# Sliding-window attention in a two-layer trunk: the emptying of its PSUM banks moved ahead in the instruction order

## The chip, the cores and the metric

The kernel runs on one core of a Trainium2 chip. The metric is the device time of one execution in microseconds (us). One core has a matrix engine (TensorE, PE in the profile; its weight loads are PEld), a vector engine (VectorE, DVE), an activation engine (ScalarE, ACT), GpSimd (POOL) and SyncE (SP). TensorE writes its results into PSUM banks, and ScalarE or VectorE copies them out to the on-chip memory SBUF; here such a copy is called an eviction.

## The reference

Input and output are 512 tokens of 1024 features in float32. Each of two layers computes:

```python
h = rmsnorm(x, norm_mix)
z = h @ w_in       # q, k, v of attention; q, k, v, o and gates of the mLSTM; gates A and B
# branch A: 8 query heads over 2 key/value heads of 64, RMS-norm and partial rotary on q and k
scores = einsum('bnqhgd,bnkhd->bnhgqk', qb, kb) * hd**-0.5   # blocks of 128 queries, own and previous block
scores = where(kpos >= 0 & kpos <= qpos & qpos - kpos < 128, scores, -inf)
m = maximum(max(scores), sink);  p = exp(scores - m)
probs = p / (sum(p) + exp(sink - m))
att = einsum('bnhgqk,bnkhd->bnqhgd', probs, vb)
# branch B: hm = chunkwise mLSTM with output gate
mixed = sigmoid(g_a) * (att @ w_att_branch) + sigmoid(g_m) * (hm @ w_m_branch)
x = x + mixed @ w_out
u = relu(rmsnorm(x, norm_ffn) @ w_ff1);  x = x + (u * u) @ w_ff2
```

## The kernel before

Each layer is built by `mixer` (everything up to `mixed @ w_out`) and `mlp`. Float32 products are made of split parts: a matrix is split into a rounded high part and the rest (`h`, `lo`; `wh`, `wl` for weights), and `mm3` issues three products, high by high, high by rest, rest by high. A weight chunk is loaded, and then split by ScalarE (L166) and VectorE (L167). The projections work on 512-column products (`mm` tiles) that collect in five PSUM banks, got from `bank()`.

Attention does not have a stage of its own. It runs as side steps between the projections' products, in 4 blocks of 128 queries by 2 key/value groups, written (b, kv) below. Each side step has a place on a list (`side`), counted in steps of products. Its PSUM space is a second pool of three banks, got from `aux()`, through which all of these pass in turn:

- `q_tr(b)`, `k_tr(b)`: transposes of the queries and keys of a block; evictions with the gains at L585/L586 (queries) and L563 to L566 (keys).
- `att_scores(b, kv, hp)`: scores of two of the group's four heads against the previous and own block; ScalarE copies the previous block's half (L604; for block 0 a fill, L602), VectorE copies the own half under the causal mask (L605, a predicated copy).
- `att_softmax(b, kv)`: works on SBUF only; maximum (L612, VectorE), four exponentials (L618, ScalarE), the sink's exponential (L620), sum and reciprocal (L621, L622), normalising multiplication over 128x512 (L623, VectorE).
- `att_probs(b, kv)`: four transposes (L52) of the normalised weights into one bank, which `split` empties into a high part (L176, ScalarE) and the rest (L177, VectorE). GpSimd masks copies of both for the previous block.
- `att_out(b, kv)`: two or four products with the values into one bank; ScalarE copies the lower half (L649), VectorE adds the head pairs with two additions (L653), and the result is split again (L656, L657).

All matrix products carry line L47 (`pe.matmul`), all transposes L52. The order of the instructions on each engine is fixed when the program is built: a scheduler goes through what is ready and takes it by priority, which normally follows the order of the code. Code under `tc.high_priority()` is put ahead of all else that is ready; `tc.high_priority(n)` raises it by n places. Before the change the raised work includes the weight loads and the weight splits (`lead[0] = 64` within attention). On the chip each engine then runs its own list from first to last, and waits where something isn't there yet.

Of the kernel before, what the change touches and what calls it, by code (L numbers as in the profile page):

```python
# [9 lines left out]
F32R = mybir.dt.float32r  # L10
BF16 = mybir.dt.bfloat16
I32 = mybir.dt.int32
AF = mybir.ActivationFunctionType
ALU = mybir.AluOpType
AX = mybir.AxisListType

P = 128
# [11 lines left out]
NEG = -1.0e30  # L29
# [4 lines left out]
def hybrid_kernel(ctx, tc, x, norm_mix, w_in, att_q_norm, att_k_norm, att_sinks, m_gate_bias,  # L34
# [3 lines left out]
    ve, sc, gp = nc.vector, nc.scalar, nc.gpsimd  # L38
# [23 lines left out]
    def nm(s):  # L62
        uid[0] += 1
        return f"{s}_{uid[0]}"
# [8 lines left out]
    def slot(dt=F32, shape=(P, T)):  # L73
        return now["act"].tile(list(shape), dt, tag="a", name=nm("a"))

    def temp(dt=F32):
        return now["tmp"].tile([P, T], dt, tag="t", name=nm("t"))
# [14 lines left out]
    def aux(shape=(P, T)):  # L92
        return now["paux"].tile(list(shape), F32, tag="aux", name=nm("aux"))
# [4 lines left out]
    def f32(ap):  # L98
        return ap.bitcast(F32)
# [72 lines left out]
    def split(src, scale=None, get=lambda: slot(F32R)):  # L172

        h, lo = get(), get()
        if scale is None:
            last_split[0] = sc.activation(h, src, AF.Copy)  # L176
            last_split[1] = ve.tensor_tensor(lo, src, f32(h), op=ALU.subtract)  # L177
        else:
            last_split[0] = sc.activation(h, src, AF.Copy, scale=scale)  # L179
            last_split[1] = ve.scalar_tensor_tensor(lo, src, scale, f32(h), op0=ALU.mult, op1=ALU.subtract)  # L180
        return h, lo
# [207 lines left out]
    def mixer(l, norm, late, order, phase):  # L389
# [116 lines left out]
        for b in range(NB):  # L506
# [5 lines left out]
                         op=ALU.mult)  # L512
# [15 lines left out]
        for i, v_ in enumerate((v4[:, :NB - 1], dv4)):  # L528
            sc.activation(v2[:, i, :, :, 0, :], v_, AF.Copy, scale=0.5)
            ve.scalar_tensor_tensor(v2[:, i, :, :, 1, :], v_, 0.5, f32(v2[:, i, :, :, 0, :]), op0=ALU.mult,  # L530
                                    op1=ALU.subtract)
# [17 lines left out]
        tri_i = tri_l.bitcast(I32)  # L549
# [21 lines left out]
        def q_tr(b):  # L571


            ps = aux()
            for j in range(4):
                pe.transpose(ps[:, j * P:(j + 1) * P], q_tok[b][:, j * P:(j + 1) * P], ident)
            for j in range(2):
                qT[b, j] = temp(F32R)
                t4 = qT[b, j].rearrange("p (i n t) -> p i n t", n=2, i=2)
                p4 = ps[:, 2 * j * P:2 * (j + 1) * P].rearrange("p (n t) -> p n t", n=2)  # L580
                for i in range(2):
                    r = slice(64 * i, 64 * i + 64)
                    o = slice(64 - 64 * i, 128 - 64 * i)
                    g = gcols[0][r, l:l + 1]
                    sc.activation(t4[r, i], p4[r], AF.Copy, scale=g)  # L585
                    ve.scalar_tensor_tensor(t4[o, i], p4[r], g, f32(t4[r, i]), op0=ALU.mult,  # L586
                                            op1=ALU.subtract)

        def att_scores(b, kv, hp):
            if hp == 0:  # L590
                sps[b, kv] = temp()
            ps = aux()
            for i in range(2):
                c = 2 * i + hp
                lhs = qT[b, kv][:, c * P:(c + 1) * P]
                o = ps[:, i * 2 * P:(i + 1) * 2 * P]
                pe.matmul(o, lhs, kTh[:, kv, b * P:(b + 2) * P], start=True, stop=False)
                pe.matmul(o, lhs, kTl[:, kv, b * P:(b + 2) * P], start=False, stop=True)
            p4 = ps.rearrange("p (h w k) -> p h w k", h=2, w=2)
            dst = sps[b, kv][:, hp * 2 * P:(hp + 1) * 2 * P].rearrange("p (h k) -> p h k", h=2)  # L600
            if b == 0:
                gp.memset(dst, NEG)  # L602
            else:
                sc.activation(dst, p4[:, :, 0, :], AF.Copy)  # L604
            ve.copy_predicated(dst, tri_i.unsqueeze(1).to_broadcast([P, 2, P]), p4[:, :, 1, :])  # L605

        def att_softmax(b, kv):
            sp = sps[b, kv]
# [16 lines left out]
        def att_probs(b, kv):  # L625
            sp = sps[b, kv]
            pt = aux()
            for i in range(4):
                pe.transpose(pt[:, i * P:(i + 1) * P], sp[:, i * P:(i + 1) * P], ident)
            hl = split(pt, get=lambda: temp(F32R))  # L630
            parts[b, kv] = [(hl, v2[:, 0, max(b - 1, 0), kv])]
            if b > 0:


                own = [temp(F32R) for _ in hl]
                for src, dst in zip(hl, own):
                    s3, d3 = (t.rearrange("p (h q) -> p h q", h=4) for t in (src, dst))
                    gp.affine_select(out=d3, in_=s3, compare_op=ALU.is_ge, fill=0.0, base=0,
                                     pattern=[[0, 4], [1, P]], channel_multiplier=-1)
                parts[b, kv].append((own, v2[:, 1, b - 1, kv]))  # L640

        def att_out(b, kv):
            po = aux()
            ls = parts[b, kv]
            for n, (pr, vb) in enumerate(ls):
                for m, p_ in enumerate(pr):
                    pe.matmul(po, vb.rearrange("p i d -> p (i d)"), p_, start=n + m == 0, stop=n == len(ls) - 1 and m == 1)
            low, both = temp(), temp()
            sc.activation(low[0:64, :], po[64:128, :], AF.Copy)  # L649
            p4, l4 = (t[0:64, :].rearrange("p (j i t) -> p j i t", j=2, i=2) for t in (po, low))  # L650
            b3 = both[:, 0:2 * P].rearrange("p (j t) -> p j t", j=2)
            for i in range(2):
                ve.tensor_tensor(b3[64 * i:64 * i + 64], p4[:, :, i, :], l4[:, :, i, :], op=ALU.add)  # L653
            for j in range(2):
                dh, dl = (a[:, b * P:(b + 1) * P] for a in att_acts[2 * kv + j])
                sc.activation(dh, b3[:, j, :], AF.Copy)  # L656
                ve.tensor_tensor(dl, b3[:, j, :], f32(dh), op=ALU.subtract)  # L657
# [182 lines left out]
        for i, (b, kv) in enumerate(units):  # L840
            at = 7 + 1.65 * i
            side += [(at, lambda b=b, kv=kv: att_scores(b, kv, 0)),
                     (at + 1.25, lambda b=b, kv=kv: att_scores(b, kv, 1)),
                     (at + 1.25, lambda b=b, kv=kv: att_softmax(b, kv)),
                     (at + 3.45, lambda b=b, kv=kv: att_probs(b, kv)),
                     (at + 3.45 + 2.2, lambda b=b, kv=kv: att_out(b, kv))]
            if kv == 0 and b + 1 < NB:
                if b + 2 < NB:
                    side += [(at + 1, lambda b=b: k_vec(b + 2)), (at + 1, lambda b=b: q_vec(b + 2))]
                side += [(at + 2 * 1.65 - 1.75, lambda b=b: k_tr(b + 1)), (at + 2 * 1.65 - 2.15, lambda b=b: q_tr(b + 1))]  # L850
# [830 lines left out]
```

## Time and profile before

| | us |
|---|---|
| median of 3 runs | 1278.73 (1278.52 to 1278.82) |
| the profiled execution | 1278.95 |
| its span in the trace | 1277.3 |
| outside the span | 1.65 |
| TensorE busy | 1266.9 (99%) |
| VectorE busy | 1040.4 (81%) |
| ScalarE busy | 793.3 (62%) |
| GpSimd busy | 256.9 (20%) |

The rows are sums over one profiled execution. Engines run side by side, so their times don't add up to the span. Attention of layer 0 lies between about 69 and 133 us of the span, that of layer 1 between about 702 and 766 us. A row of a timeline gives the start, the length, the engine, the line in the kernel, the operation and its tiles with output before input, and in brackets how long the engine had stood idle before it and which work ended that.

### The profile page before, as it was taken

The page shows a single profiled execution, that of the slowest core. Times are in us where ns is not written, and L with a number is a line of the kernel's source. Part 1 is how long each engine was busy: PE and PEld are TensorE (multiplying, and loading weights), DVE is VectorE, ACT ScalarE, POOL GpSimd, SP SyncE. Part 2 cuts the span into 40 slices and gives each one's busy share as a digit, 9 for nine tenths or more (in the row PEclk, how much of TensorE's full clock was granted, in tenths as well). Part 3 has the DMA queues.
Part 4 walks back from the last instruction along what each step waited for, and adds up shares of the span by engine and source line. Part 5 has one row for each costly group of instructions (what it writes and reads, how often), then busy time and mean ns, then how long its engine had stood idle before and what let it go on. Part 6 is the DMA issues. An engine that isn't in the chain of part 4 may idle for free.

```text
span 1277.3 us, 19227 instructions
## 1 busy us (share of the span) xinstructions
PE 1266.9 (99%) x6882; PEld 1088.6 (85%) x6882; DVE 1040.4 (81%) x1654; ACT 793.3 (62%) x1399; POOL 256.9 (20%) x337
## 2 busy tenths in 40 slices
PE   9999999999999999999999999999999999999998
PEld 7877888888889999999888778888888899999987
DVE  4689988688787887969957889876887879879697
ACT  5578579645665666656554885785455656565563
POOL 4513132021003031130114031310300120301210
PEclk9999999999999999999999999999999999999999
DMA  5426372567569898898224254634756697988953
GB/s 157 113 59 158 106 132 75 157 125 156 173 166 208 220 184 213 198 206 214 34 75 117 60 155 108 116 108 139 144 146 185 166 227 187 203 215 191 215 144 99
DMA packets 138927, 193.35 MB, mean 151 GB/s; under 512 B 10568, under 2 KB 79024, under 8 KB 138832
## 3 DMA queue, kind: packets, MB, share of 16 engines
q1 hardware_dynamic: 92992, 129.72, 33.3%
q0 software_dynamic: 45120, 62.00, 30.2%
q8 instruction: 54, 0.88, 0.3%
q10 hardware_dynamic: 720, 0.40, 0.1%
q14 instruction: 41, 0.34, 0.1%
HBM read 188.95 MB, written 2.10 MB: 150 GB/s over the span
## 4 chain that ended last, share of the span: by engine, by line
PE 89%; ACT 5%; DVE 3%; DMA 2%; issue 1%; DVEq 0%; SPq 0%; ACTq 0%
PE mm L47 72%; PE aux L47 14%; PE aux L52 2%; DMA w<-in_w_in_dram 1%; DVE wl L167 1%; ACT t L618 1%; ACT wh L166 1%; ACT t L585 0%; DVE t L653 0%; ACT p L703 0%; DVE t L586 0%; DVE t L177 0%; ACT t L176 0%; DMA x<-in_x_dram 0%; DMA w<-in_w_m_branch_dram 0%
## 5 line engine op out<-in xcount | busy, mean ns | idle before, releaser
L47 PE MATMUL mm<-i,wh 128*128 128x512 f32 (+1 forms) x1280 | 353.6, 363 | 0.0
L1162 ACT ACTIVATE wh<-raw 128x1024 fp32r<-128x1024 f32 x212 | 223.2, 1056 | 178.8 <-PE mm L47 91.8
L1163 DVE TENSOR_TENSOR wl<-raw,wh 128x1024 fp32r<-128x1024 f32 x212 | 255.7, 1221 | 81.0 <-ACT wh L1162 80.8
L47 PEld LDWEIGHTS mm<-i,wh 128*128 128x128 f32 x1280 | 223.2, 189 | 30.4
L47 PE MATMUL mm<-i,wl 128*128 128x512 f32 (+1 forms) x640 | 229.0, 358 | 0.0
L47 PE MATMUL mm<-wh,uh 128*128 128x512 f32 x440 | 171.8, 390 | 0.0
L47 PE MATMUL mm<-wl,uh 128*128 128x512 f32 x440 | 171.7, 390 | 0.0
L47 PE MATMUL mm<-wh,ul 128*128 128x512 f32 x440 | 171.2, 389 | 0.0
L1332 POOL DMA_DIRECT2D raw<-in_w_ff_dram x48 | 62.6, 1311 | 381.2 <-DMA raw<-in_w_ff_dram 246.3
L47 PEld LDWEIGHTS mm<-i,wl 128*128 128x128 f32 x640 | 120.9, 189 | 18.0
L167 DVE TENSOR_TENSOR wl<-w,wh 128x512 fp32r<-128x512 f32 (+1 forms) x144 | 97.3, 678 | 42.9 <-ACT wh L166 42.1
L166 ACT ACTIVATE wh<-w 128x512 fp32r<-128x512 f32 (+1 forms) x144 | 86.4, 604 | 67.4 <-PE mm L47 49.7
L47 PE MATMUL mm<-wh,i 128*128 128x512 f32 (+1 forms) x352 | 101.0, 360 | 1.0 <-ACT wh L166 0.6
L47 PEld LDWEIGHTS mm<-wh,ul 128*128 128x128 f32 x440 | 82.6, 188 | 17.4
L1217 DVE SCALAR_TENSOR_TENSOR x<-mm,ms,x 128x512 f32<-128x512 f32 x126 | 90.6, 745 | 8.1 <-PE mm L47 8.1
L47 PEld LDWEIGHTS mm<-wh,uh 128*128 128x128 f32 x440 | 82.8, 188 | 16.1
L47 PEld LDWEIGHTS mm<-wl,uh 128*128 128x128 f32 x440 | 82.8, 188 | 15.5
L1489 POOL DMA_DIRECT2D raw<-in_w_ff_dram x36 | 43.3, 1204 | 150.6 <-DVE wl L1163 114.9
L47 PEld LDWEIGHTS mm<-wh,i 128*128 128x128 f32 x352 | 62.0, 188 | 11.7 <-ACT i L179 1.1
L47 PE MATMUL aux<-i,wh 128*128 128x256 f32 x384 | 69.5, 283 | 0.0
L47 PE MATMUL aux<-t,wh 128*128 128x256 f32 x384 | 69.5, 283 | 0.0
L47 PE MATMUL mm<-wl,i 128*128 128x512 f32 (+1 forms) x176 | 61.9, 352 | 0.0
(317 smaller groups left out, 2519.4 us busy)
## 6 DMA issues: line engine op xcount, KB each, us to landing
raw<-in_w_ff_dram SPq DMA_DIRECT2D x144, 512.0 KB, 5.0
raw<-in_w_ff_dram POOLq DMA_DIRECT2D x84, 512.0 KB, 8.0
w<-in_w_in_dram SPq DMA_DIRECT2D x112, 256.0 KB, 2.7
a<-in_w_in_dram POOLq DMA_DIRECT2D x32, 256.0 KB, 5.8
qa<-in_w_out_dram POOLq DMA_DIRECT2D x12, 512.0 KB, 5.9
a<-in_w_in_dram SPq DMA_DIRECT2D x16, 256.0 KB, 4.2
w<-in_w_att_branch_dram SPq DMA_DIRECT2D x16, 256.0 KB, 2.8
w<-in_w_m_branch_dram SPq DMA_DIRECT2D x16, 256.0 KB, 2.9
```

Source lines behind the costliest of these rows:

```text
L47: latest[0] = nc.tensor.matmul(*args, **kw)
L52: latest[0] = nc.tensor.transpose(*args)
L166: sc.activation(wh[:, :off], raw[:, :off], AF.Copy)
L167: ve.tensor_tensor(wl[:, :off], raw[:, :off], f32(wh[:, :off]), op=ALU.subtract)
L618: sc.activation(s3[:, i, :], s3[:, i, :], AF.Exp, bias=m[:, i:i + 1], accum_out=den[:, i:i + 1])
L1162: sc.activation(hi, src, AF.Copy)
L1163: ve.tensor_tensor(lo, src, f32(hi), op=ALU.subtract)
L1217: ve.scalar_tensor_tensor(xh[:, cc], ps[i][:, cc], ms[j][:, b:b + 1], xh[:, cc], op0=ALU.mult, op1=ALU.add)
L1332: gp.dma_start(to[h], src(h, i, j), accum_op=ALU.add)
L1489: gp.dma_start(to[h], src(h, i, j), accum_op=ALU.add)
```

## The change

Four groups of evictions of the three auxiliary banks are put under `tc.high_priority()`: those of `q_tr`, of `att_scores`, of `att_probs` and of `att_out`. The evictions of `k_tr`, the softmax and the last split of `att_out` stay as they were.

```diff
@@ q_tr
-                    sc.activation(t4[r, i], p4[r], AF.Copy, scale=g)
-                    ve.scalar_tensor_tensor(t4[o, i], p4[r], g, f32(t4[r, i]), op0=ALU.mult,
-                                            op1=ALU.subtract)
+                    with tc.high_priority():
+                        sc.activation(t4[r, i], p4[r], AF.Copy, scale=g)
+                        ve.scalar_tensor_tensor(t4[o, i], p4[r], g, f32(t4[r, i]), op0=ALU.mult,
+                                                op1=ALU.subtract)
@@ att_scores
-            if b == 0:
-                gp.memset(dst, NEG)
-            else:
-                sc.activation(dst, p4[:, :, 0, :], AF.Copy)
-            ve.copy_predicated(dst, tri_i.unsqueeze(1).to_broadcast([P, 2, P]), p4[:, :, 1, :])
+            with tc.high_priority():
+                if b == 0:
+                    gp.memset(dst, NEG)
+                else:
+                    sc.activation(dst, p4[:, :, 0, :], AF.Copy)
+                ve.copy_predicated(dst, tri_i.unsqueeze(1).to_broadcast([P, 2, P]), p4[:, :, 1, :])
@@ att_probs
-            hl = split(pt, get=lambda: temp(F32R))
+            with tc.high_priority():
+                hl = split(pt, get=lambda: temp(F32R))
@@ att_out
-            sc.activation(low[0:64, :], po[64:128, :], AF.Copy)
             p4, l4 = (t[0:64, :].rearrange("p (j i t) -> p j i t", j=2, i=2) for t in (po, low))
             b3 = both[:, 0:2 * P].rearrange("p (j t) -> p j t", j=2)
-            for i in range(2):
-                ve.tensor_tensor(b3[64 * i:64 * i + 64], p4[:, :, i, :], l4[:, :, i, :], op=ALU.add)
+            with tc.high_priority():
+                sc.activation(low[0:64, :], po[64:128, :], AF.Copy)
+                for i in range(2):
+                    ve.tensor_tensor(b3[64 * i:64 * i + 64], p4[:, :, i, :], l4[:, :, i, :], op=ALU.add)
```

The instructions are the same in number and kind; their places on the engines' lists differ, in attention of both layers and in the same way. The lines of the changed kernel are shifted: L585 is 586, L604/L605 are 606/607, L618 to L623 are 620 to 625, L649 is 655, L653 is 657, L656/L657 are 660/661.

The first place is the softmax of block 1, group 0 in layer 0 (about 88 to 95 us). `t_1013` is its tile of weights with the sums `den_1092`, `aux_1131` the bank of the transposes of the unit before, `aux_1146` that of an `att_out`, `aux_1170` and `aux_1198` banks of scores, `kT_623` the keys, `w_1359` a weight chunk. ScalarE's list before:

```order
L618 ACTIVATE t_1013,den_1092<-t_1013,m_1087 128x128 x4
L620 ACTIVATE es_1090<-es_1090 128x4
L563 ACTIVATE kT_623<-aux_1104,gc_147 64x128
L564 ACTIVATE kT_623<-aux_1104,gc_147 64x128
L176 ACTIVATE t_1136<-aux_1131 128x512
L166 ACTIVATE wh_1361<-w_1359 128x512
L649 ACTIVATE t_1149<-aux_1146 64x512
L604 ACTIVATE t_1114<-aux_1170 128x256
```

And ScalarE's list there now:

```order
L620 ACTIVATE t_1013,den_1092<-t_1013,m_1087 128x128 x2
L176 ACTIVATE t_1136<-aux_1131 128x512
L620 ACTIVATE t_1013,den_1092<-t_1013,m_1087 128x128
L655 ACTIVATE t_1149<-aux_1146 64x512
L620 ACTIVATE t_1013,den_1092<-t_1013,m_1087 128x128
L622 ACTIVATE es_1090<-es_1090 128x4
L563 ACTIVATE kT_623<-aux_1104,gc_147 64x128
L564 ACTIVATE kT_623<-aux_1104,gc_147 64x128
L606 ACTIVATE t_1114<-aux_1170 128x256
L660 ACTIVATE a_632<-t_1150 128x128
L166 ACTIVATE wh_1361<-w_1359 128x512
```

The evictions of `aux_1131` and `aux_1146` now stand between the exponentials of `t_1013`, and the weight split L166 has moved back. VectorE's list at the same place, before:

```order
L621 TENSOR_TENSOR den_1092<-den_1092,es_1090 128x4
L622 RECIPROCAL den_1092<-den_1092 128x4
L623 TENSOR_TENSOR t_1013<-t_1013,den_1092 128x512
L565 SCALAR_TENSOR_TENSOR kT_623<-aux_1104,gc_147,kT_623 64x128
L177 TENSOR_TENSOR t_1137<-aux_1131,t_1136 128x512
L566 CAST kT_623<-kT_623 64x128
L653 TENSOR_TENSOR t_1150<-aux_1146,t_1149 64x256 x2
L605 COPY_PREDICATED t_1114<-tri_l,aux_1170 128x256
```

And VectorE's list there now:

```order
L177 TENSOR_TENSOR t_1137<-aux_1131,t_1136 128x512
L657 TENSOR_TENSOR t_1150<-aux_1146,t_1149 64x256 x2
L623 TENSOR_TENSOR den_1092<-den_1092,es_1090 128x4
L624 RECIPROCAL den_1092<-den_1092 128x4
L565 SCALAR_TENSOR_TENSOR kT_623<-aux_1104,gc_147,kT_623 64x128
L607 COPY_PREDICATED t_1114<-tri_l,aux_1170 128x256
L625 TENSOR_TENSOR t_1013<-t_1013,den_1092 128x512
L566 CAST kT_623<-kT_623 64x128
```

The split of `aux_1131`, the additions on `aux_1146` and the predicated copy on `aux_1170` stood behind the normalising multiplication of `t_1013`; all three stand ahead of it now.

The second place is TensorE's list some ten us later, as the difference of the two lists (minus before, plus now). `mm` tiles are products of the projections, `aux_1307` is a bank for scores of block 1, group 1, and `aux_1317` takes the transposes of that block's group 0, `t_1114`:

```order
 L47 MATMUL mm_936<-i_277,wl_1290 128x512
 L47 MATMUL mm_958<-i_277,wh_1289 128x512
+L47 MATMUL aux_1307<-kT_623,t_1072 128x256 x4
 L47 MATMUL mm_958<-i_278,wh_1289 128x512
 L47 MATMUL mm_958<-i_277,wl_1290 128x512
```

and further on:

```order
 L47 MATMUL mm_1393<-i_115,wh_1361 128x512
 L47 MATMUL mm_1393<-i_114,wl_1362 128x512
-L47 MATMUL aux_1307<-kT_623,t_1072 128x256 x4
 L47 MATMUL mm_1397<-i_114,wh_1361 128x512
 L47 MATMUL mm_1397<-i_115,wh_1361 128x512
 L47 MATMUL mm_1397<-i_114,wl_1362 128x512
 L47 MATMUL mm_1358<-i_114,wh_1411 128x512
+L52 MATMUL aux_1317<-ident,t_1114 128x128 x4
```

The scores `aux_1307` have moved ahead by eleven products, and the transposes `aux_1317` ahead as well.

The third place is VectorE's list around the softmax of block 2, group 1 (`t_1306`, sums `den_1384`); `aux_1437` is the bank of an `att_out`, `aux_1463` and `aux_1491` are banks of scores, `m_1470` takes the maximum of the next unit. Before:

```order
L621 TENSOR_TENSOR den_1384<-den_1384,es_1382 128x4
L622 RECIPROCAL den_1384<-den_1384 128x4
L623 TENSOR_TENSOR t_1306<-t_1306,den_1384 128x512
L653 TENSOR_TENSOR t_1443<-aux_1437,t_1442 64x256 x2
L605 COPY_PREDICATED t_1401<-tri_l,aux_1463 128x256
L605 COPY_PREDICATED t_1490<-tri_l,aux_1491 128x256
```

And now:

```order
L607 COPY_PREDICATED t_1401<-tri_l,aux_1463 128x256
L657 TENSOR_TENSOR t_1443<-aux_1437,t_1442 64x256
L607 COPY_PREDICATED t_1490<-tri_l,aux_1491 128x256
L657 TENSOR_TENSOR t_1443<-aux_1437,t_1442 64x256
L623 TENSOR_TENSOR den_1384<-den_1384,es_1382 128x4
L614 TENSOR_REDUCE m_1470<-t_1401 128x4
L624 RECIPROCAL den_1384<-den_1384 128x4
L661 TENSOR_TENSOR a_637<-t_1443,a_636 128x128
L625 TENSOR_TENSOR t_1306<-t_1306,den_1384 128x512
```

The additions, both predicated copies and the next unit's maximum have gone ahead of the multiplication.

## The prediction

> **What bounds the kernel now.** I read the page's head first, then its busy times and the chain of work that ended last.
>
> ```profile
> span 1277.3 us, 19227 instructions
> PE 1266.9 (99%) x6882; PEld 1088.6 (85%) x6882; DVE 1040.4 (81%) x1654; ACT 793.3 (62%) x1399; POOL 256.9 (20%) x337
> PE 89%; ACT 5%; DVE 3%; DMA 2%; issue 1%; DVEq 0%; SPq 0%; ACTq 0%
> ```
>
> TensorE is busy for 99% of the span, and the chain runs over it for 89%. A reordering that removes no matmul can only win where TensorE stands still: 1277.3 − 1266.9 = 10.4 us in the whole kernel. The next question is how much of this lies where the change moves anything. By the order of instructions, the first row that moves on ScalarE, VectorE or TensorE in layer 0 is one that ran at about 86 us, and the last that matters at about 133; in layer 1 the same rows move between 718 and 765. The table of stretches gives start:end, length, then busy time of PE, PEld, DVE, ACT and POOL, the granted clock, the DMA share and GB/s:
>
> ```profile
> 69.50:85.80 16.30, 15.42 (x85) 12.86 (x84) 13.93 (x35) 11.25 (x35) 0.00 (x0) 1.00 0.22 60
> 85.80:133.00 47.20, 45.79 (x227) 36.08 (x226) 41.16 (x106) 39.87 (x121) 11.92 (x16) 1.00 0.47 124
> 133.00:260.00 127.00, 127.00 (x627) 105.93 (x626) 106.07 (x250) 86.79 (x204) 23.96 (x39) 1.00 0.49 117
> 718.00:765.50 47.50, 46.07 (x229) 36.35 (x228) 41.43 (x107) 40.17 (x121) 12.06 (x16) 1.00 0.49 125
> ```
>
> In the moved stretch PE is idle for 47.20 − 45.79 = 1.41 us of layer 0 and 47.50 − 46.07 = 1.43 of layer 1. Beside it VectorE is busy for 41.16 / 47.20 = 87% and ScalarE for 84%: both are almost full there, so what is put first on them puts something else last. The clock is 1.00, so it decides nothing. From 133 to 260 PE records no idle time at all: a layer that leaves attention late by some tenths stays late, and one that leaves early stays early. What PE waited for, over the whole run (total us, times, longest):
>
> ```profile
> PE aux L52 <- DVE t L653: 1.7, 4, 0.5
> PE aux L47 <- DVE t L605: 1.3, 2, 0.7
> PE aux L47 <- DVE t L653: 0.5, 2, 0.2
> PE aux L52 <- ACT wh L166: 0.3, 2, 0.2
> ```
>
> The 1.7 and 0.5 are waits for an auxiliary bank (three of them) until the head-pair additions of `att_out`, L653, have emptied it. The change aims at these. The 1.3 are waits at the scores for a predicated copy, L605. The prioritised rows include L605, but these two waits (85.24 us in layer 0) lie ahead of the first moved row, in the stretch from 69.50 that loses 16.30 − 15.42 = 0.88 us, so they stay. TensorE's timeline around the waits (start, length, engine, line, operation, tiles; in brackets the wait and who ended it):
>
> ```profile
> 85.24 0.74 PE L47 MATMUL aux<-kT,t 128*128 128x256 f32 x4 [0.67 <-DVE t L605]
> 92.72 0.39 PE L47 MATMUL mm<-i,wh 128*128 128x512 f32 x1
> 93.53 0.63 PE L52 MATMUL aux<-ident,t 128*128 128x128 f32 x4 [0.42 <-DVE t L653]
> 99.11 0.40 PE L47 MATMUL mm<-i,wl 128*128 128x512 f32 x1
> 99.96 0.30 PE L52 MATMUL aux<-ident,kvi 128*128 128x128 f32 x1 [0.45 <-DVE t L653]
> 104.82 0.61 PE L47 MATMUL mm<-i,wh 128*128 128x512 f32 x2
> 105.27 0.39 PE L47 MATMUL mm<-i,wl 128*128 128x512 f32 x1
> 108.22 0.39 PE L47 MATMUL mm<-i,wh 128*128 128x512 f32 x1
> 108.72 0.66 PE L52 MATMUL aux<-ident,t 128*128 128x128 f32 x4
> 113.60 0.40 PE L47 MATMUL mm<-i,wl 128*128 128x512 f32 x1
> 114.23 0.94 PE L47 MATMUL aux<-t,v 128*128 128x512 f32 x3 [0.23 <-DVE t L653]
> 124.78 0.39 PE L47 MATMUL mm<-i,wl 128*128 128x512 f32 x1
> 125.34 0.63 PE L52 MATMUL aux<-ident,t 128*128 128x128 f32 x4 [0.17 <-ACT wh L166]
> ```
>
> Unhindered, a 512-column product starts (105.27 − 104.82) / 2 = 0.225 us after the one before, though each row is 0.39 long. So the true loss at a wait is the distance of two starts less 0.225, and it is larger than the recorded idle: at 93.53 it is 93.53 − 92.72 − 0.225 = 0.58, at 99.96 0.62, at 108.72 0.27, at 114.23 0.40, at 125.34 0.33. Together 2.20 us for layer 0, against 1.41 of recorded idle. That is the most the change can recover per layer.
>
> **The change part by part.** It adds and removes no instruction; work and transfers are the same, and only places in the queues move. On POOL and SyncE two masks and one weight load move past transfers that are needed tens of us later: nothing. Weight splits are moved back behind evictions on ScalarE and VectorE; the split of a weight is needed about 8 us after it (the last one at risk ends at 116.9 and TensorE first reads it at 124.78), so this costs nothing while the delay is under that:
>
> ```profile
> 116.20 0.68 DVE L167 TENSOR_TENSOR wl<-w,wh 128x512 fp32r<-128x512 f32 x1
> ```
>
> What has no such cover is the softmax. Its exponentials (L618), its sum, reciprocal and normalising multiplication (L623) are not raised, and TensorE's next transposes (L52) read what L623 writes. These rows of before show the first place at which the order differs much, ScalarE first, then VectorE; what follows is a replay by hand: the new order, with these durations.
>
> ```profile
> 88.09 0.40 ACT L618 ACTIVATE t<-t,m 128x128 f32<-128x128 f32 x1
> 89.65 0.19 ACT L620 ACTIVATE es<-es 128x4 f32<-128x4 f32 x1
> 90.63 0.60 ACT L176 ACTIVATE t<-aux 128x512 fp32r<-128x512 f32 x1
> 91.25 0.63 ACT L166 ACTIVATE wh<-w 128x512 fp32r<-128x512 f32 x1
> 91.91 0.59 ACT L649 ACTIVATE t<-aux 64x512 f32<-64x512 f32 x1
> 94.20 0.60 ACT L176 ACTIVATE t<-aux 128x512 fp32r<-128x512 f32 x1 [0.47 <-PE aux L52]
> 90.28 0.69 DVE L623 TENSOR_TENSOR t<-t,den 128x512 f32<-128x512 f32 x1
> 91.40 0.69 DVE L177 TENSOR_TENSOR t<-aux,t 128x512 fp32r<-128x512 f32 x1
> 92.54 0.85 DVE L653 TENSOR_TENSOR t<-aux,t 64x256 f32<-64x256 f32 x2 [0.20 <-ACT t L649]
> ```
>
> *Transposes of block 1, group 0 (93.53).* In before the multiplication ended at 90.97, the bank was free at 93.39 when the second addition ended (92.54 + 0.85), and the bank decided. After: two exponentials, L176 (0.60), one exponential, L649 (0.59), the last exponential and the small one. From 88.09 that puts L649 at 90.0 to 90.6 instead of 91.91, and the small exponential's end at 91.1 instead of 89.84. On VectorE the additions end at 91.5, 1.9 us sooner. Sum, reciprocal, one k step and one predicated copy come next, and then the multiplication at 92.6 to 93.3, 2.3 us later than before. TensorE arrives at 93.0, with one more product (0.225) behind it, and starts at about 93.36: it loses 0.37 instead of 0.58. The bank wait has become a data wait. Counting start and product, TensorE is ahead by 0.17 + 0.23 = 0.40.
>
> *The transpose at 99.96.* The bank is that of another `att_out`; its additions move ahead of the multiplication that stood in front of them (98.36, below), and they end about 1.9 us sooner, at 97.9 with TensorE's arrival at 98.9. The wait of 0.62 goes: ahead by 1.02. The rows of this and of the later places:
>
> ```profile
> 98.36 0.69 DVE L623 TENSOR_TENSOR t<-t,den 128x512 f32<-128x512 f32 x1
> 98.97 0.84 DVE L653 TENSOR_TENSOR t<-aux,t 64x256 f32<-64x256 f32 x2
> 117.64 0.69 DVE L623 TENSOR_TENSOR t<-t,den 128x512 f32<-128x512 f32 x1
> 118.25 0.84 DVE L653 TENSOR_TENSOR t<-aux,t 64x256 f32<-64x256 f32 x2
> 119.12 0.78 DVE L605 COPY_PREDICATED t<-tri_l,aux 128x256 f32<-128x256 int32 x2
> 119.24 0.63 PE L52 MATMUL aux<-ident,t 128*128 128x128 f32 x4
> ```
>
> *Scores pulled forward.* The order puts the second scores of block 1, group 1 (aux_1307) some eleven products earlier on TensorE. The bank they take is freed by a predicated copy behind a weight split and the first gate products of VectorE; that copy ends at about 101.0 by the replay, TensorE is there at 100.62 and loses 0.42. The scores of block 2 (aux_1402) come soon after and wait 0.35 for the k part of that block, whose evictions (L563 to L566) aren't raised.
>
> *The later transposes.* At 117.64 the multiplication preceded the additions (118.25) and two predicated copies (119.12); now it follows them and a reduce over a tile of its own size. That is 0.84 + 0.78 + 0.69 = 2.3 us of other work put in front; part of that runs while the exponentials are going on anyway, and in before the multiplication ended 0.9 us ahead of its transposes (at 117.64 + 0.69 = 118.33, against a start at 119.24). I get a loss of 0.52 there. The same working gives 0.58 for block 2, group 0 (108.72 in before), 0.28 for block 3, group 0 (0.33 at 125.34 in before) and 0.25 for its group 1.
>
> *The sum.* Lost per layer in before: 2.20. Lost after: 0.37 + 0.42 + 0.35 + 0.58 + 0.52 + 0.28 + 0.25 = 2.77. That is +0.57. Following TensorE's own position step by step instead, it leaves the last `att_out` of attention 0.40 late, because some of the new losses shorten the next. I take the middle, 0.49, for each of two layers: +1.0 us. The profiled execution took 1278.95, of which 1.65 lie outside the span; with the change 1279.95. The median of the runs is 0.22 under the profiled one, so the forecast is 1279.7. Each of some ten placements of a wait is known to about 0.3 us, independent of the others: about 1 us per layer; as both layers have the same order, the errors add, to 2 us. Its own range is 1277.7 to 1281.3.
>
> A rule that would speak for the change: the Trainium skill, "Perfetto Trace Analysis", section "Optimization Strategy", says that a gap repeating over a stretch of the busiest engine can mean too little PSUM for the next tile. By that rule all bank waits would go and the sum would be rival A's; the trace agrees that L653 ends six of the waits.
>
> **The rivals.** *A, faster: the waits simply go.* The evictions come sooner and the softmax is ready in time all the same. For it: the bank waits at 99.96 and 114.23 had their data long before. Against it: VectorE at 87%, and 2.3 us of delay for L623 at the first transposes alone. It gives 1278.95 − 2 × 2.20 − 0.22 = 1274.3; by recorded idle only, 1278.95 − 1.41 − 1.43 − 0.22 = 1275.9. I take the middle, 1275.1.
>
> *B, slower: the multiplication L623 falls further behind than I worked out.* The mechanism is the queue: an eviction at the head of ScalarE or VectorE whose bank isn't filled yet holds up the exponentials and multiplications behind it. The row at 94.20 shows it in before: L176 stood 0.47 us waiting for TensorE, with a weight split queued after it. With the evictions first, such heads are more frequent, and TensorE's next transposes wait for what is held up, which fills no bank in the meantime. The price is one pass of 0.69 (L623's own size) more at three of the six transposes per layer: 3 × 0.69 × 2 = 4.1 us over the forecast, 1283.8; at all six, 1287.9. It decides from the point where the added losses pass 1.3 us per layer (1278.73 + 2.6 = 1281.3). For it: L623 stands behind L653 in every block of the new order. Against it: the losses I found are each under 0.6. The Trainium skill, "PSUM — Partial Sum Buffer", section "Engine vs sequencer instructions", states that the queues of ScalarE and VectorE are strictly first in, first out; the row at 94.20 agrees.
>
> *C, no effect:* the largest waits (85.24) are ahead of what moves, the rest cancels, 1278.7.
>
> **How the numbers follow.** A measurement of this kernel tells about 0.2%, 2.6 us, from no change: 1276.2 and 1281.3 are the limits. The forecast gets 0.53, A 0.11, B 0.32, C 0.04. B gets more than A because a softmax behind evictions stands in the order itself, while A needs room on an engine that is 87% busy. Faster 0.11 (A), same 0.57 (forecast and C), slower 0.32 (B). The range runs from A's 1275.1, with half of A below it, to 1284.5, just beyond B's price: it leaves out some 0.05 below and 0.13 above.
>
> **What would show it.** Right: the waits of `aux L52` for L653 at 93.53 and 99.96 are gone, and waits of `aux L52` for the multiplication (L625 after the shift of lines) stand in their place, five per layer of 0.2 to 0.6; the waits for the predicated copy at 72 to 86 us are as before; the idle time of 85.8 to 133 is between 1.2 and 2.5 us; the end moves by twice one layer's shift. A would show in that idle time falling under 0.5 us, B in its rising over 2.7 with ScalarE or VectorE standing at evictions. Wrong altogether: a shift that arises outside attention (a late weight, an output transfer), since I put that at nothing.

## The result, and the profile after

The changed kernel takes 1285.46 us (median of 4 runs, 1284.19 to 1285.87), the kernel before 1278.77: ratio 1.0051, 95% interval 1.0039 to 1.0063. It is 6.7 us slower. The forecast was 1279.7, and the range ended at 1284.5.

The profiled execution took 1285.18 us with a span of 1283.5, and TensorE does the same work in it. The stretches of the changed kernel (columns as before):

```profile
PE 1266.8 (99%) x6882; PEld 1087.9 (85%) x6882; DVE 1042.8 (81%) x1654; ACT 792.5 (62%) x1399; POOL 254.1 (20%) x337
69.50:85.80 16.30, 15.31 (x84) 12.64 (x82) 14.09 (x35) 11.13 (x36) 0.00 (x0) 1.00 0.22 63
85.80:133.00 47.20, 43.34 (x215) 33.93 (x216) 40.94 (x104) 38.10 (x117) 10.44 (x15) 1.00 0.46 123
133.00:260.00 127.00, 127.00 (x625) 106.02 (x624) 106.63 (x252) 88.14 (x207) 23.17 (x39) 1.00 0.48 117
```

TensorE's idle time in the stretch of the change has grown from 1.41 to 47.20 − 43.34 = 3.86 us, and it gets through 215 products there instead of 227. VectorE and ScalarE are busy for less time too: no engine has become fuller, all of them wait. Measured from the first scores of a layer (first row `aux<-kT,t`) to the first row `aux<-ones,lf` behind attention, layer 0 takes 78.20 us against 75.51 and layer 1 78.54 against 75.05, so +2.69 and +3.49, where +0.49 was forecast for each. Their sum, 6.18, is all but 0.05 of the difference between the two profiled spans. What TensorE waited for:

```profile
PE aux L52 <- DVE t L625: 6.5, 10, 2.2
PE aux L47 <- DVE t L607: 2.1, 4, 0.8
PE aux L47 <- DVE kT L565: 1.3, 2, 0.6
```

The waits for the additions have gone, and waits for the multiplication (now L625) stand in their place, five per layer, as forecast; but they sum to 6.5 us, and two of them lie far above the 0.2 to 0.6 that was forecast for each. TensorE's timeline shows which of them are large:

```profile
93.92 0.33 PE L52 MATMUL aux<-ident,t 128*128 128x128 f32 x1 [0.18 <-DVE t L625]
101.63 0.39 PE L47 MATMUL aux<-kT,t 128*128 128x256 f32 x1 [0.19 <-DVE t L607]
109.76 0.50 PE L47 MATMUL aux<-kT,t 128*128 128x256 f32 x2 [0.63 <-DVE kT L565]
114.22 0.52 PE L52 MATMUL aux<-ident,t 128*128 128x128 f32 x3 [0.33 <-DVE t L625]
120.75 0.63 PE L52 MATMUL aux<-ident,t 128*128 128x128 f32 x4 [0.36 <-DVE t L625]
127.88 0.63 PE L52 MATMUL aux<-ident,t 128*128 128x128 f32 x4 [1.46 <-DVE t L625]
132.08 0.63 PE L52 MATMUL aux<-ident,t 128*128 128x128 f32 x4 [0.59 <-DVE t L625]
763.64 0.63 PE L52 MATMUL aux<-ident,t 128*128 128x128 f32 x4 [2.19 <-DVE t L625]
```

By the distance of starts the loss is 0.16 to 0.17 more than each bracket. At 127.88, block 3, group 0, it is 1.62 us in layer 0, and 2.35 at the same place in layer 1 (763.64). The chain of waits, followed back from there (start, length, what):

```profile
114.35 0.61 DVE wl L167
114.97 0.02 SPq L155
115.02 6.88 DMA w<-in_w_in_dram
121.98 0.10 ACT wh L166
122.52 0.48 ACT t L620 x2
```

The chain leaves the bank evictions altogether. A weight chunk, issued at 115.02, lands after 6.88 us. ScalarE has its split L166 at the head of its list and waits 2.48 us for it, and the exponentials of block 3 (L620) stand right behind the split. (Of the 2.48 us, 0.71 would be there anyway: in the run below with the transfers out of the way, the same split waits that long for TensorE.)

```profile
121.98 0.63 ACT L166 ACTIVATE wh<-w 128x512 fp32r<-128x512 f32 x1 [2.48 <-DMA w<-in_w_in_dram]
```

The weight itself is needed much later. In the kernel before, the same chunk was issued at 113.39 and landed after 2.6 us, and its split came 5 us after that, without a wait for it:

```profile
DMA to landing us min/median/max: 2.6/2.6/2.6
121.08 0.63 ACT L166 ACTIVATE wh<-w 128x512 fp32r<-128x512 f32 x1 [0.52 <-PE mm L47]
```

Two things differ. The chunk is issued 1.6 us later, since VectorE's split L167 of an earlier chunk, which frees its buffer (first row of the chain above), now ends at 114.95 instead of 113.32. And the transfer itself takes longer. The rows of SyncE and GpSimd tell why; first before:

```profile
100.94 3.28 SPq L718 DMA_DIRECT2D a<-in_w_in_dram  x7
111.50 15.19 SPq L155 DMA_DIRECT2D w<-in_w_in_dram  x6
104.14 0.93 POOL L734 DMA_DIRECT2D a<-in_w_in_dram  x1 [6.64 <-DMA a<-in_w_in_dram]
105.72 2.65 POOL L734 DMA_DIRECT2D a<-in_w_in_dram  x3 [0.65 <-DMA a<-in_w_in_dram]
```

And after:

```profile
101.03 1.85 SPq L722 DMA_DIRECT2D a<-in_w_in_dram  x4
110.50 0.33 SPq L155 DMA_DIRECT2D w<-in_w_in_dram  x1
110.87 1.57 SPq L722 DMA_DIRECT2D a<-in_w_in_dram  x3
107.69 1.36 POOL L641 TENSOR_SCALAR_AFFINE_SELECT t<-t 128x512 fp32r<-128x512 f32 x2 [10.35 <-ACT t L176]
109.00 3.62 POOL L738 DMA_DIRECT2D a<-in_w_in_dram  x4
```

SyncE used to issue seven loads of later weights (tiles `a`) in a row at 101 to 104 us. Now a weight chunk whose buffer becomes free only at 110.50 stands ahead of the last three, and they go out at 110.9 to 111.9. GpSimd used to issue its four accumulating transfers (they add what they load to an `a` tile) at 104 to 107; now two masks stand ahead of them, and they go at 109 to 111. Six of these seven are still in flight when the chunk of 115.02 is issued (one landed at 113.41, the others at 116.95 to 121.22).

### The profile page after: what moved, and what is told of

Its sections match the earlier page's. It is cut to its first block, busy times and chain, and to the rows that moved or that the text cites. A ratio compares the mean times of both kernels' runs of the same rounds, so it can differ in the third digit from the quotient of the medians.

```text
span 1283.5 us, 19235 instructions
## 1 busy us (share of the span) xinstructions
PE 1266.8 (99%) x6882; PEld 1087.9 (85%) x6882; DVE 1042.8 (81%) x1654; ACT 792.5 (62%) x1399; POOL 254.1 (20%) x337
## 4 chain that ended last, share of the span: by engine, by line
PE 90%; DVE 4%; ACT 3%; DMA 2%; issue 1%; ACTq 0%; DVEq 0%; SPq 0%
PE mm L47 74%; PE aux L47 14%; PE aux L52 2%; DMA w<-in_w_in_dram 2%; ACT t L620 1%; DVE wl L167 1%; DVE m L614 1%; DVE t L607 0%; DVE t L625 0%; ACT t L586 0%; DVE t L587 0%; DVE t L657 0%; DMA grow<-in_norm_mix_dram 0%; ACT p L707 0%; DVE a L661 0%
## 5 line engine op out<-in xcount | busy, mean ns | idle before, releaser
L167 DVE TENSOR_TENSOR wl<-w,wh 128x512 fp32r<-128x512 f32 (+1 forms) x144 | 95.9, 669 | 45.3 <-ACT wh L166 43.5
L166 ACT ACTIVATE wh<-w 128x512 fp32r<-128x512 f32 (+1 forms) x144 | 86.6, 604 | 69.4 <-PE mm L47 47.6
```

Of the source, the lines that this page charges most:

```text
L166: sc.activation(wh[:, :off], raw[:, :off], AF.Copy)
L167: ve.tensor_tensor(wl[:, :off], raw[:, :off], f32(wh[:, :off]), op=ALU.subtract)
```

## The experiments

Theory T: the excess is the late chunk, whose split stands at the head of ScalarE's list. Rival R: raised evictions hold up the softmax by themselves, in lists that are served strictly in order, and transfers play no part. In the column of edits, "before" is the kernel before with an edit, "after" the changed kernel with an edit. The table has all runs; the two columns of attention are the measure above, less that of before, in us; the last is ScalarE's wait for a weight chunk in attention, both layers, read from its timeline.

| run | edit | median us | ratio to before | attention, layers 0, 1 | ScalarE's wait for chunks |
|---|---|---|---|---|---|
| after | the change | 1285.46 | 1.0051 | +2.69, +3.49 | 2.48, 3.60 |
| defer_after | after, the seven transfers later | 1284.50 | 1.0041 | +1.36, +1.39 | none |
| loads_first | after, the three loads earlier | 1281.56 | 1.0023 | +1.39, +1.60 | 0, 1.65 |
| late_before | before, transfers as in after | 1280.17 | 1.0010 | +0.31, +0.71 | none |
| defer_before | before, the seven transfers later | 1285.51 | 1.0050 | +0.02, +0.01 | none |
| out_only | before, att_out raised | 1278.77 | 0.9999 | +0.09, +0.15 | none |
| probs_only | before, att_probs raised | 1281.33 | 1.0022 | +0.54, +1.80 | none |
| softmax_only | before, softmax raised | 1284.38 | 1.0046 | +1.65, +2.73 | 1.84, 2.84 |
| out_softmax | before, att_out and softmax raised | 1277.56 | 0.9993 | −0.78, −0.35 | none |
| probs_out_softmax | before, att_probs, att_out and softmax raised | 1283.68 | 1.0039 | +2.35, +2.19 | 2.62, 2.42 |
| softmax_too | after, softmax raised too | 1287.25 | 1.0065 | +1.97, +6.12 | 3.00, 5.44 |
| no_masks | after, without masks | 1277.89 | 0.9995 | −0.90, −0.35 | none |
| no_masks_before | before, without masks | 1277.01 | 0.9987 | −1.37, −0.95 | none |

**The transfers put behind the chunks of attention, in both kernels.**

```diff
         def begin(k):
             wa[k] = slot()
-            load(wa[k], 0, 0, k)
-            gp.dma_start(wa[k], block(0, 1, k), accum_op=ALU.add)
+            with tc.issue_after(asked[0].ins):      # the last weight chunk asked for
+                load(wa[k], 0, 0, k)
+            with tc.issue_after(masks[3, 1].ins):   # the last mask of attention
+                gp.dma_start(wa[k], block(0, 1, k), accum_op=ALU.add)
...
-            load(wb[k], 1, 1, k)
+            with tc.issue_after(asked[0].ins):
+                load(wb[k], 1, 1, k)
```

> The changed kernel, with the seven loads of the summed weights (tiles a) and their four accumulating transfers put behind the weight chunks of attention; the lists of TensorE, VectorE and ScalarE stay word for word those of the changed kernel. Theory T (transfers): in the changed kernel these eleven-odd transfers are in flight when the weight chunk issued at 115.02 is loaded, so it lands after 6.88 us instead of 2.6, ScalarE's split waits 2.48 us for it at the head of the queue, and the exponentials of block 3 wait behind it; this makes 1.62 of the loss at 127.88 and 2.35 at 763.64, where 0.3 was worked out, and 0.75 instead of 0.25 at the next transposes. T expects that chunk to land in under 3.5 us, the two losses to fall to 0.3 to 0.6, and the time to fall by 3 to 4.5 us to 1281 to 1282.5. Rival R (the queue of evictions alone holds up the softmax, transfers don't matter): 1285.5 as before, losses at 127.88 and 763.64 unchanged.

The chunk landed after 2.7 us, and the two losses fell to 0.31 and 0.32 us, close to what the prediction had worked out for this place (0.28):

```profile
126.34 0.52 PE L52 MATMUL aux<-ident,t 128*128 128x128 f32 x3 [0.15 <-DVE t L625]
```

Attention took 1.3 and 2.1 us less than in the changed kernel. The total fell by only 1 us, to 1284.50 (interval of the ratio 1.0028 to 1.0053), which missed the 1281 to 1282.5 of T. The control tells why:

> The kernel before with the same transfers put behind the weight chunks of attention, as a control for the first run. In before the weight chunks of this stretch land in 2.6 to 3.7 us, so there is next to nothing to win: T and R both expect 1278.3 to 1279.0. Over 1279.5 would mean that the later transfers are missed by their readers at about 157 us, and that the first run has to be read with that cost.

It took 1285.51 (1.0037 to 1.0063), attention unchanged (+0.02, +0.01), and the loss lies behind it. It isn't that the deferred transfers are missed by their readers, as the expectation had it: no wait for a tile `a` is recorded on ScalarE or VectorE. They now delay the chunks of the next weight (the one issued at 137.81 took 6.99 us, in the kernel before 2.63), and the same thing happens again: its split at the head of ScalarE's list waits, 4.95 us in layer 0 and 4.60 in layer 1, and behind it stands an eviction (L801) that TensorE waits for.

```profile
144.91 0.63 ACT L166 ACTIVATE wh<-w 128x512 fp32r<-128x512 f32 x1 [4.95 <-DMA w<-in_w_att_branch_dram]
PE mm L47 <- ACT t L801: 3.2, 2, 1.8
PE mm L47 <- DVE p L920: 0.9, 1, 0.9
```

So the deferral has a price of its own, the control's expectation was wrong, and the first run's total says nothing; its attention does.

**The three loads put back, nothing else.** The list of SyncE is that of before; TensorE, ScalarE and GpSimd keep the lists of the changed kernel, and VectorE's differs only from 139 us on, behind attention.

```diff
-        side += [(24.5 + 0.5 * k, lambda k=k: begin(k)) for k in range(4)]
-        side += [(28.0 + 0.5 * k, lambda k=k: begin_other(k)) for k in range(4)]
+        side += [(21.5 + 0.01 * k, lambda k=k: begin(k)) for k in range(4)]
+        side += [(21.55 + 0.01 * k, lambda k=k: begin_other(k)) for k in range(3)]
+        side += [(29.5, lambda: begin_other(3))]
...                # and the next weight chunk is issued behind the third of these loads
```

> The changed kernel with SyncE's list put back to that of before: the three a loads ahead of the weight chunk that waits for its buffer, so they are issued at about 103 instead of 110.9 to 111.9. The lists of TensorE, ScalarE and GpSimd stay those of the changed kernel (the four accumulating transfers still go at 109 to 111); VectorE's moves only behind attention. T: with three of the seven transfers out of the way the chunk issued at 115.02 takes about 4 us instead of 6.88 and lands at about 119, before ScalarE is ready for its split; the losses of 1.62 and 2.35 fall to 0.3 to 0.5, and 1281.3 to 1282.8 is left (the part that is not transfers: 1.36 per layer). If the accumulating transfers alone hold the chunk up, it still takes 6 us or more and the time stays at 1284 to 1285.5.

Measured 1281.56 (1.0014 to 1.0032), within what T said. The chunk takes 5.0 us (T said about 4), and ScalarE doesn't wait for it in layer 0; in layer 1 it waits 1.65 us for two chunks. TensorE's losses at block 3, group 0 are 0.31 and 0.48 us. This is the cleanest test: four rows of SyncE's list in each layer are worth 3.9 of the 6.7 us by the medians, 3.2 by attention in the profiled executions.

```profile
126.71 0.52 PE L52 MATMUL aux<-ident,t 128*128 128x128 f32 x3
DMA to landing us min/median/max: 5.0/5.0/5.0
```

**The late transfers alone.** The lists of TensorE, VectorE and ScalarE are those of before.

```diff
+            with tc.issue_after(masks[1, 1].ins):              # behind the masks of block 1
+                gp.dma_start(wa[k], block(0, 1, k), accum_op=ALU.add)
...
+            with tc.high_priority(), tc.issue_after(requests[ahead[0]].ins):   # the chunk that waits for its buffer
+                load(wb[k], 1, 1, k)
```

> The kernel before, with only the transfers in the order of the changed kernel: three a loads behind the weight chunk that waits for its buffer, the four accumulating transfers behind the masks of block 1. The lists of TensorE, VectorE and ScalarE stay word for word those of before. T expects the chunk that took 2.61 us (issued at 113.39) to take 5 us or more and its split, at 117.99 in before, to wait 1.5 to 2.5 us for it; TensorE then loses 0.5 to 2 us per layer that it did not lose, 1279.8 to 1282.8. R expects 1278.8.

The time, 1280.17 (1.0000 to 1.0019, so hardly told from no change), lies in T's range, but not by T's mechanism. The chunk did land late:

```profile
L155 SPq DMA_DIRECT2D w<-in_w_in_dram x1: 339/339/339, 112.8 to 112.8; - x1
DMA to landing us min/median/max: 7.3/7.3/7.3
```

Yet ScalarE never waited for it. The expectation had the wrong row for its split, 117.99; it is the next one, 121.08 in before, and 121.36 here, after the chunk has landed (112.83 + 7.3 = 120.1). What TensorE lost anew, 0.54 us at the transposes of 119.50, it lost to VectorE: beside two masks of GpSimd at 114.47 to 117.02 a weight split of VectorE took 1.49 us instead of 0.69 (the last section has more of this), and the multiplication and the additions (L655) came behind it.

```profile
116.09 1.49 DVE L168 TENSOR_TENSOR wl<-w,wh 128x512 fp32r<-128x512 f32 x1
119.50 0.52 PE L52 MATMUL aux<-ident,t 128*128 128x128 f32 x3 [0.37 <-DVE t L655]
```

So T needs both of its parts: a late chunk alone costs little (here), and a split at the head costs little when its chunk is there (the three loads put back). The changed kernel has both, and there the chunk was also issued 2.2 us later than here.

**Which evictions matter.**

```diff
+            with tc.high_priority():
                 sc.activation(low[0:64, :], po[64:128, :], AF.Copy)
                 for i in range(2):
                     ve.tensor_tensor(...)
```

> The kernel before with only the evictions of att_out raised (the copy and the two additions), which are the ones TensorE waited for. SyncE's order is that of before, three of four accumulating transfers too. T: no collision, so the bank waits of 0.58, 0.62 and 0.40 go and part comes back as waits for the multiplication: 1277.0 to 1279.5. R: the multiplication is pushed back by the additions alone, 1280 to 1283.

Measured 1278.77 (0.9990 to 1.0008): no change, as T said. The bank waits it was meant to remove are partly replaced by waits for predicated copies (L605, 3.1 us in all against 1.3). The first of the bank waits stays, 0.58 us at 93.21.

> The kernel before with only the evictions of att_probs raised (the split of the transposed weights). On SyncE a weight chunk then stands ahead of three a loads as in the changed kernel, on GpSimd masks and accumulating transfers keep the order of before. If the three a loads are what delays the chunk, T expects the chunk to take over 4 us and a loss for it, 1280 to 1282; if the accumulating transfers are what matters, the chunk takes 2.6 to 4 us and the time is 1278.5 to 1280. R expects 1280 to 1283 (multiplication put off by this split alone).

Measured 1281.33 (1.0013 to 1.0031). The chunks took up to 6.4 us, but no wait of ScalarE for one is recorded, so T's mechanism is not shown here, and the time lies in R's range too. Layer 1 lost more than layer 0 (1.80 against 0.54). A part of that shows in the trace: in layer 1 three masks of GpSimd ran back to back at 747.48 to 749.67, and two additions of VectorE beside them took 1.90 us, where in layer 0 they took 1.11 beside two masks; behind them TensorE lost 0.71 us at 751.05, and 0.29 at the same place of layer 0.

```profile
114.54 1.11 DVE L658 TENSOR_TENSOR a<-t,a 128x128 fp32r<-128x128 f32 x2
747.90 1.90 DVE L658 TENSOR_TENSOR a<-t,a 128x128 fp32r<-128x128 f32 x2
```

The rest stays open.

**The softmax raised.** The whole of `att_softmax` from the maximum to the multiplication goes under `tc.high_priority()`, alone and together with others.

> The changed kernel, with the softmax (maximum, exponentials, sum, reciprocal, multiplication) raised as well. SyncE and GpSimd keep the late transfers: the weight chunk still waits behind its buffer ahead of three a loads, and masks stand ahead of the accumulating transfers. On ScalarE the four exponentials of block 3, group 0 now stand ahead of the split of the chunk that lands late (in the changed kernel: behind it). T: the chunk lands late as before (5 us or more), but nothing of the softmax stands behind its split; the loss at the transposes of block 3, group 0 falls from 1.62 and 2.35 to under 0.5, and those for the multiplication elsewhere (0.36, 0.49, 0.52, 0.75) shrink: 1277.5 to 1280.5. R in the form that VectorE is full and something must come last: what is put off now are the key parts and weight splits, TensorE waits for these instead, 1281 to 1285.

This expectation failed: 1287.25 (1.0052 to 1.0079), slower still. The exponentials did go ahead of that split, but another split came to stand ahead of two evictions (a score eviction, L606, and the split L176 of transposed weights), and its chunk was later yet:

```profile
119.17 0.63 ACT L166 ACTIVATE wh<-w 128x512 fp32r<-128x512 f32 x1 [3.00 <-DMA w<-in_w_in_dram]
119.83 0.38 ACT L606 ACTIVATE t<-aux 128x256 f32<-128x256 f32 x1
756.49 0.63 ACT L166 ACTIVATE wh<-w 128x512 fp32r<-128x512 f32 x1 [5.44 <-DMA w<-in_w_in_dram]
758.05 2.08 PE L47 MATMUL aux<-t,v 128*128 128x512 f32 x4 [3.42 <-DVE t L607]
```

What T had right is the blocker, what it had wrong is that the softmax is what stands behind it.

> The kernel before with only the softmax raised, no eviction. GpSimd's list is that of before, SyncE's differs by one place. It separates the run with att_out and softmax raised (1277.56): if the softmax alone gives that gain, 1277 to 1278; if the gain came from the evictions of att_out, which need the softmax not to be put off, 1278.3 to 1280.

1284.38 (1.0033 to 1.0058): neither of the two, with the same blocker (1.84 and 2.84 us).

> The kernel before with only the evictions of att_out and the softmax raised; SyncE's and GpSimd's lists are those of before, so no transfer moves. T: the bank waits of 0.62 and 0.40 go and the multiplication isn't put off, the time falls by 1 to 3 us to 1275.8 to 1278. R: VectorE is full, other evictions (the predicated copies) come late instead, 1278.5 to 1281.

1277.56 (0.9985 to 1.0002): the shortest time of all with the full computation, 0.9 us under the runs of before beside it, but not told from no change. No chunk is waited for in attention.

> The kernel before with att_probs, att_out and the softmax raised; q and scores not. SyncE's list is nearly that of before, so T expects no late chunk: 1276.5 to 1278.5, a candidate to beat both kernels. R (VectorE full, something comes last): 1279 to 1282.

1283.68 (1.0027 to 1.0052), the expectation of T failed here too, by the same blocker (2.62 and 2.42 us): SyncE's list was "nearly" that of before, with one chunk ahead of two loads, and this was enough.

**Without the masks.**

```diff
-                own = [temp(F32R) for _ in hl]
-                for src, dst in zip(hl, own):
-                    ...gp.affine_select(...)
-                parts[b, kv].append((own, v2[:, 1, b - 1, kv]))
+                parts[b, kv].append((hl, v2[:, 1, b - 1, kv]))
```

> The changed kernel without the masks of the previous block's weights on GpSimd (left out: the masking, so previous-block keys outside the window count too). Claim: two masks that run back to back (1.36 us) stretch VectorE's operations with SBUF operands beside them, the cast of the keys L566 from 0.22 to 0.68 and the sum L623 from 0.16 to 0.55, and this makes the loss at the second block's scores 0.79 instead of 0.35 and that at the last transposes 0.75 instead of 0.25. Without masks the casts take 0.21 to 0.23 and the sums 0.16, and these two losses fall to 0.3 to 0.45 and 0.2 to 0.4; 1.5 to 2 us of the whole, 1283 to 1284 if the late chunk stays, less if its transfers move too. The rival for these two (they are plain queueing behind evictions) expects them unchanged at 0.79 and 0.75.

This kernel and the next leave out the window's mask, so keys outside the window count. 1277.89 (0.9986 to 1.0004): the two losses are 0.36 and none. But the lists moved as well, and the late chunk with them, so the 7.6 us are not the price of the masks.

> The kernel before without the masks of the previous block's weights on GpSimd (left out: the masking), as control for the run without masks of the changed kernel. In before the masks run singly, and they stretch a cast or a sum only where nobody waits for it: 1277.8 to 1279.0. If it falls by as much as the changed kernel did without them (7 us), the masks cost both the same and say nothing of the change.

1277.01 (0.9978 to 0.9996), a fall of 1.7 us and more than expected: before pays for its masks too. What the changed kernel pays for them these two runs don't tell.

## Why the prediction was wrong, step by step

- *What bounds it, and where:* right. Nothing moved outside attention, the clock stayed at 1.00, the idle time arose where it was looked for (3.86 us there, beyond the 2.5 that the prediction allowed), and the wait at 85.74 stayed (0.84 us, 0.67 in before).
- *"Bank waits become waits for the multiplication":* right in kind, and in size at four of seven places, a fifth once the chunk is out of the way. Losses per place, forecast and measured in layer 0: 0.37 and 0.35 (93.92), 0.42 and 0.36 (101.63), 0.58 and 0.49 (114.22), 0.52 and 0.52 (120.75); 0.28 and 1.62 (127.88), or 0.31 with the transfers out of the way.
- *"On POOL and SyncE two masks and one weight load move past transfers that are needed tens of us later: nothing":* **this is the step that failed.** I priced the moved transfers by when their own readers need them. They cost by what is in flight beside them: the chunk of 115.02 took 6.88 us instead of 2.6, and ScalarE's list stood for it. This makes 1.3 us of layer 0 and 2.1 of layer 1, by the run with the transfers out of the way (2.69 − 1.36, 3.49 − 1.39).
- *"Weight splits … costs nothing":* failed with it. The cover was TensorE's need of the weight, about 8 us later, and that held. But in a list that is served in order a split that waits holds up all behind it, and its own reader says nothing about them. A later split also frees its buffer later: that is why this chunk was issued 1.6 us later.
- *The size of two terms:* the wait for the keys (0.35, measured 0.79) and the last transposes (0.25, measured 0.75), together +0.94 per layer. With 0.49 that gives 1.43, and 1.36 to 1.60 is what is left in the two runs where the transfers are moved away. Rows for these two, and what made them larger, are in the last section.
- *Rival B* had the sign and nearly the size (1283.8), and a list whose head waits is its mechanism; but its head was to be an eviction whose bank isn't filled. It was a weight split whose chunk hasn't landed, which the row at 94.20 could not have shown: in before no split in attention waited for a chunk. That its price comes near is luck: it was added up from passes of 0.69 us at three places per layer, and one place per layer made most of the loss. The sign set for B came half true: the idle time rose over 2.7 us, but ScalarE stood at a weight split and not at an eviction.

R as stated falls: with the lists of the three engines unchanged up to the end of attention, the order of the transfers alone makes 3.9 us. It keeps what stays, some 1.4 us per layer: the 0.49 that was forecast, and two terms that were too small.

## What to carry to other kernels

When a scheduler reorders, read every queue, above all the DMA issues, and ask of each moved transfer what it will share the wire with, not only when its reader comes. Then look at the head of each in-order list for an instruction that waits for a transfer: what stands behind it is the price, whatever the instruction itself is needed for. Where the helper engines are over 80% busy, as VectorE and ScalarE are in this stretch, raising one group of instructions brings another set of waits: of the seven choices tried here, the change among them, none came out under the kernel before by more than the runs vary.

## What the runs showed of the hardware

**VectorE beside GpSimd.** In the changed kernel the keys' cast L566 takes 0.22 us at 89.60, 93.90 and 112.20; beside the two masks of 107.69 to 109.05 it took 0.68, and ended 0.08 us after them. The sum of the softmax (L623 in this kernel), 0.16 us elsewhere, took 0.55 beside the masks of 129.62, and ended with those at 131.0. VectorE and GpSimd in the changed kernel:

```profile
108.45 0.68 DVE L566 CAST kT<-kT 64x128 fp32r<-64x128 f32 x1
109.35 0.36 DVE L565 SCALAR_TENSOR_TENSOR kT<-aux,gc,kT 64x128 fp32r<-64x128 f32 x1
130.45 0.55 DVE L623 TENSOR_TENSOR den<-den,es 128x4 f32<-128x4 f32 x1 [0.17 <-ACT es L622]
129.62 1.36 POOL L641 TENSOR_SCALAR_AFFINE_SELECT t<-t 128x512 fp32r<-128x512 f32 x2 [4.66 <-ACT t L176]
107.66 0.69 DVE L177 TENSOR_TENSOR t<-aux,t 128x512 fp32r<-128x512 f32 x1
```

L177, which reads a PSUM bank, ran beside the same masks in its usual 0.69; in the twelve traces with masks, 54 such splits began beside a mask, and none took over 0.70. In the two kernels without masks no cast in attention took over 0.28 us and no sum over 0.17. So the stretch is shown. Single masks do it too: in before a mask at 121.54 took 1.09 us, and the small addition L615 beside it 0.59 instead of 0.15. What the change adds is two masks back to back, as it evicts both halves of the transposed weights together, at places where TensorE waits. VectorE goes from the cast at 108.45 over another small addition to L565 at 109.35 with no idle time, and TensorE's scores at 109.76 wait for that L565. From the sum at 130.45 it goes over the reciprocal to the multiplication, and the transposes at 132.08 wait for that. Less the stretches of 0.46 and 0.39 us, the two losses of 0.79 and 0.75 would be 0.33 and 0.36 (an estimate), near the 0.35 and 0.25 of the forecast. The run without masks agrees (0.36 and none), but its lists moved too, so the shares are worked out from the chain and not tested alone. The Trainium skill, "SBUF — State Buffer", section "SBUF: two separate sides", states that VectorE, in operations with two SBUF inputs (against a GpSimd operation that reads SBUF) or in a two-port mode, and GpSimd share a pair of ports under an exclusive lock, and that the later one blocks fully. The rows agree: the stretched operations end with the masks, or shortly after.

**The clock after a pause.** Where TensorE stood 3.42 us (758.05 of the run with the softmax raised too), it ran at a granted clock of 0.52 for the next 3.4 us; the pause of 2.19 us in the changed kernel left it at 1.00. In those 3.4 us products start 0.43 us apart (at 759.92, 760.35 and 760.78) instead of 0.225, so a part of that run's +6.12 us in layer 1 is the slow clock.

```profile
758.00:761.40 3.40, 3.35 (x8) 2.70 (x9) 2.53 (x6) 2.62 (x13) 1.26 (x2) 0.52 0.42 91
763.60:767.00 3.40, 3.36 (x17) 2.75 (x17) 2.27 (x8) 3.09 (x12) 1.27 (x2) 1.00 0.32 77
```

The Trainium skill, "TensorE: Matmul & The Clock Gate", section "What's actually happening", puts the change to half the clock after an idle window of about 3.4 us; these two rows agree.
